# The down projection of an encoder block: tokens as rows of its result, and the last norm per row

## The chip, the core and the metric

One core of a Trainium2 chip runs the whole block; the metric is the time of one execution in microseconds. Five engines work side by side: TensorE (PE, matmuls; PEld its weight loads), VectorE (DVE), ScalarE (ACT), GpSimd (POOL) and SyncE (SP). Each works through its own list in order. Transfers between the chip's memory (SBUF) and the device memory are issued from such a list too, mostly SP's, and carried by 16 transfer engines. PSUM is where TensorE writes its sums.

## What is computed

```python
# x: (1, 2048, 1024) float32, one layer
h = rmsnorm(x, norm_mix_pre)
...                                   # input projection, two branches, gates, w_o
x = x + rmsnorm(merged @ w_o, norm_mix_post)         # "x1" in the kernel
h = rmsnorm(x, norm_mlp_pre)
f = square(relu(h @ w_up)) @ w_down                  # (2048,1024) @ (1024,4096) @ (4096,1024)
x = x + rmsnorm(f, norm_mlp_post)                    # rmsnorm over the 1024 channels of a token
```

## The kernel before

Activations lie in SBUF with channels on the 128 partitions and tokens along the row. Every float32 operand of a matmul is split in two parts of TensorE's type, a high part (a cast on ScalarE, `wh`, `fo` or `big`) and a low part (what is left, a subtraction on VectorE, `wl` or `tr`), and a product is three passes: high by high, high by low, low by high. Where a low part was made once and kept, it is loaded again instead.

The down projection (`down` in the trace) runs at the end, over four slabs `s` of 1024 hidden channels, each for two blocks `b` of 1024 tokens. A slab's product is cut in two by two halves of 512 (result channels by hidden channels by tokens) and made from seven half-size products `i` in place of eight, from sums and differences of the halves. `weights_down` makes the weights of product `i` as two tiles `o` of 128x1024; `token_cells` makes its activations as two cells (hi, lo); `down_product` runs it: for `o` in (0, 1), `product` contracts with the weight tile as the stationary operand and the cells as the moving one, 24 matmuls of 128x512 into a PSUM tile of 128x1024, whose rows are result channels and whose columns are tokens. So a weight tile is done with after its own 24 matmuls. The sums over slabs are kept in `acc` (`big` in the trace): in slab 0 ScalarE copies, later VectorE adds. The order of products is `DOWN` in slabs 0 to 2, where both blocks use one set of weights, and `DOWN_LAST` in the last slab, where it is all of b=0, then all of b=1, and where the weights are loaded again for the second block: sums from `wsum`, low parts from `lows`, both written to device memory earlier. Tiles come from pools with few buffers: three for `wh`, three for `wl`, nine for `tr`, 28 for `big`.

The last norm and the addition of x1 are the class `Finish`, one for each block b and token half t (512 tokens). Its squares are made on ScalarE (`Squares`), summed over partitions by TensorE with a column of 1/D (`root_pe`, `root_acc`, L458), the inverse root is taken on VectorE (`root_dve`), and TensorE spreads it over the partitions again (`spread_pe`, L542 and L548, tile `rb`). Then come a multiplication, an addition of x1 (on VectorE, GpSimd, or by an adding transfer) and the store of the cell. `fin[0,0]`, `fin[0,1]` and `fin[1,0]` run beside later products. The last, `fin[1,1]`, is `at_end` and `first_squares`: it follows the last product, with seven idle matmuls (L469) in between.

What sets the order: the program is written out in one list, and `Lane` objects give out steps of background work after every product half (`bg`); `high_priority` moves loads and casts ahead of their use, and `ordered` and `mark` tie the products in a row. Each engine's list follows from that, and a tile waits for its buffer to come free.

Of the kernel before, what the change touches and what calls it, by code (L numbers as in the profile page):

```python
# [45 lines left out]
C_MPOST = 40  # L46
C_CNT = 48
# [13 lines left out]
IDLE = (28, 7)  # L61
# [7 lines left out]
def block_kernel(  # L69
# [11 lines left out]
    params: bass.AP,  # L81
    out: bass.AP,
# [110 lines left out]
    fd, lod = {}, {}  # L193
# [289 lines left out]
    def root_dve(st, e=None, mean=None):  # L483
# [7 lines left out]
        if mean is not None:  # L491
            nc.vector.tensor_scalar(a, st, mean, EPS, op0=ALU.mult, op1=ALU.add)
        elif e is None:
            nc.vector.tensor_scalar(a, st, EPS, None, op0=ALU.add)
        else:
            add(a, st, e)
# [192 lines left out]
    def first_octet():  # L689
# [53 lines left out]
        with tc.high_priority(offset=URGENT), in_turn():  # L743
# [7 lines left out]
            idle(IDLE[0], root_psum())  # L751
# [815 lines left out]
    ENDS = {(1, 0): 4, (0, 0): 2, (1, 1): 5, (0, 1): 3}  # L1567
# [125 lines left out]
    chains = {}  # L1693

    def down_product(s, i, b, w, cells):
        for o in (0, 1):
            if s < LAST:
                ps = psum("down")
                product(ps, w[o], cells)
                if s == 0:  # L1700
                    acc[i, o, b] = mk(*BIG)
                    mark(nc.scalar.copy(acc[i, o, b], ps))
                else:
                    a = acc[i, o, b]
                    mark(add(a, a, ps))
            else:
                last_product(i, o, b, w[o], cells)
# [9 lines left out]
    def last_product(i, o, b, w, cells):  # L1717

        if i in (1, 2, 5):
            chains[i, o] = psum("down")  # L1720
        ps = chains[{1: 1, 6: 1, 7: 1, 4: 1, 2: 2, 5: 5, 3: 5}[i], o]
        product(ps, w, cells, start=i in (1, 2, 5), stop=i in (4, 2, 3))
        m, t = {1: (0, 0), 6: (0, 1), 7: (1, 1), 4: (1, 0), 2: (0, 0), 5: (1, 1), 3: (0, 1)}[i]
        c = acc[{(0, 0): 2, (0, 1): 3, (1, 0): 4, (1, 1): 5}[m, t], o, b]
        if (i, o, b) == (DOWN_LAST[-1], 1, 1):
            for h in (slice(0, T), slice(T, TB)):
                mark(add(c[:, h], c[:, h], ps[:, h]))
        else:
            mark(add(c, c, ps))
        if i == ENDS[m, t]:  # L1730
            fin[b, t].ready[2 * m + o] = c

    def beside(o, a, b):
        return nc.gpsimd.tensor_tensor(o, a, b, op=ALU.add)

    HOW = {(0, 0): "GGGG", (0, 1): "DGDG", (1, 0): "GGAD", (1, 1): "DDDD"}

    class Finish:


        def __init__(self, b, t):
            self.b, self.t, self.x, self.ready = b, t, {}, {}
            self.near = 4 if b else 3 if t else 1
            self.order = (2, 3, 0, 1)

        def how(self, c):
            return HOW[self.b, self.t][self.order.index(c)]

        def fetch(self, cells):
            for c in cells:  # L1750
                if self.how(c) != "A":
                    self.x[c] = mk(*BIG)
                    load(self.x[c], x1d[self.b, c, self.t])
# [267 lines left out]
```

## Time and profile before

| | us |
|---|---|
| median of 3 runs | 2172.24 (2170.28 to 2172.63) |
| profiled execution, its own time | 2174.1 |
| its span | 2172.3 |
| TensorE busy | 2144.8 |
| VectorE busy | 1706.2 |
| ScalarE busy | 1045.1 |

The span is the time from the first instruction of the profiled execution to the last; its own time has 1.8 us around that. The down projection starts near 1545 us and its last matmul ends near 2151 us. Matmuls overlap, so the durations of neighbours add up to more than the time that they take.

### The profile page before, as it was taken

What the parts mean: (1) busy time and instruction counts of PE and PEld (TensorE: products, weight loads), DVE (VectorE), ACT (ScalarE), POOL (GpSimd) and SP (SyncE); (2) the same over time, 40 slices, a digit from 0 to 9 for tenths busy, and PEclk for the clock granted to TensorE, in tenths of its full rate; (3) what the DMA queues carried; (4) which work ended last, traced back from release to release, by engine and by line L of the source; (5) the groups of instructions that cost most, each with busy time, mean ns of one, the idle gap of its engine ahead of it and who ended that gap; (6) DMA issues with size and microseconds to landing.
All of it is one profiled execution on the core that took longest, in us unless ns stands there. A gap on an engine that the chain in (4) does not pass through costs nothing.

```text
span 2172.3 us, 24919 instructions
## 1 busy us (share of the span) xinstructions
PE 2144.8 (99%) x9499; PEld 1772.5 (82%) x9499; DVE 1706.2 (79%) x1631; ACT 1045.1 (48%) x1102; POOL 40.0 (2%) x45
## 2 busy tenths in 40 slices
PE   9999999999999999999999999999999999999997
PEld 8788878888888888888888888888878888888886
DVE  8999787999779999997778856876654666597477
ACT  6444453334534655545635666665444322223453
POOL 0000000000000000000000000000000000000023
PEclk9999999999999999999999999999999999999998
DMA  4789998688897687435695777985956545446797
GB/s 177 259 304 331 337 353 314 223 293 290 304 348 285 249 304 271 153 117 223 230 351 213 269 273 288 342 312 219 364 197 232 184 169 180 155 137 206 257 361 259
DMA packets 161175, 561.21 MB, mean 258 GB/s; under 512 B 18704, under 2 KB 22928, under 8 KB 161040
## 3 DMA queue, kind: packets, MB, share of 16 engines
q1 hardware_dynamic: 144784, 500.38, 64.5%
q10 hardware_dynamic: 12672, 46.14, 5.5%
q0 software_dynamic: 3600, 13.11, 1.7%
q8 instruction: 74, 1.21, 0.2%
q14 instruction: 45, 0.37, 0.1%
HBM read 372.29 MB, written 187.79 MB: 258 GB/s over the span
## 4 chain that ended last, share of the span: by engine, by line
PE 88%; DVE 6%; DMA 2%; issue 2%; ACT 1%; SPq 0%; DVEq 0%; ACTq 0%
PE down L252 28%; PE up L252 28%; PE wo L252 7%; PE glu L252 6%; PE B L252 4%; PE gb L252 4%; PE A L252 4%; PE ga L252 3%; PE pool L252 3%; DVE y L910 3%; PE rb L458 1%; DVE tr L120 1%; DVE wl L123 1%; DMA kept<-ws 1%; DMA big<-xt 1%
## 5 line engine op out<-in xcount | busy, mean ns | idle before, releaser
L252 PE MATMUL up<-big,wh 128*128 128x512 f32 x1792 | 480.3, 390 | 1.4 <-DVE big L123 1.2
L252 PEld LDWEIGHTS up<-big,wh 128*128 128x128 f32 x1792 | 335.8, 188 | 71.9 <-DVE big L123 1.7
L209 ACT CAST wh<-wr 128x1024 fp32r<-128x1024 f32 x167 | 175.6, 1052 | 316.7 <-PE up L252 69.8
L252 PE MATMUL down<-tr,wh 128*128 128x512 f32 x800 | 311.5, 389 | 0.0
L910 DVE SCALAR_TENSOR_TENSOR y<-v,cst,y 128x1024 f32<-128x1024 f32 x240 | 306.9, 1279 | 2.4
L252 PE MATMUL down<-fo,wh 128*128 128x512 f32 x784 | 301.5, 390 | 1.1 <-ACT fo L1688 1.1
L252 PE MATMUL up<-big,wl 128*128 128x512 f32 x896 | 276.0, 389 | 0.0
L209 ACT CAST wh<-ws 128x1024 fp32r<-128x1024 f32 x124 | 130.6, 1053 | 223.9 <-PE up L252 75.0
L252 PE MATMUL down<-fo,wl 128*128 128x512 f32 x768 | 236.5, 389 | 0.0
L252 PEld LDWEIGHTS up<-big,wl 128*128 128x128 f32 x896 | 168.2, 188 | 35.0
L120 DVE TENSOR_TENSOR big<-big,down 128x1024 f32<-128x1024 f32 (+1 forms) x85 | 102.4, 1205 | 115.7 <-PE down L252 115.6
L1688 ACT CAST fo<-tr 128x1024 fp32r<-128x1024 f32 x86 | 86.8, 1051 | 207.6 <-PE down L252 139.4
L123 DVE TENSOR_TENSOR wl<-ws,wh 128x1024 fp32r<-128x1024 f32 x116 | 141.5, 1220 | 44.2 <-ACT wh L209 42.2
L252 PEld LDWEIGHTS down<-tr,wh 128*128 128x128 f32 x800 | 150.2, 188 | 31.1
L252 PEld LDWEIGHTS down<-fo,wh 128*128 128x128 f32 x784 | 147.2, 188 | 31.9 <-ACT fo L1688 1.6
L252 PEld LDWEIGHTS down<-fo,wl 128*128 128x128 f32 x768 | 144.2, 188 | 29.9
L123 DVE TENSOR_TENSOR wl<-wr,wh 128x1024 fp32r<-128x1024 f32 x111 | 135.1, 1218 | 28.1 <-ACT wh L209 23.2
L123 DVE TENSOR_TENSOR tr<-tr,fo 128x1024 fp32r<-128x1024 f32 x86 | 102.9, 1232 | 46.3 <-ACT fo L1688 46.3
L252 PE MATMUL glu<-big,wh 128*128 128x512 f32 x432 | 118.4, 396 | 3.9 <-ACT tr L408 3.9
L252 PE MATMUL gb<-big,wh 128*128 128x512 f32 x448 | 121.6, 393 | 0.2 <-ACT tr L408 0.2
L252 PE MATMUL wo<-big,wh 128*128 128x512 f32 x448 | 120.2, 390 | 0.0
L252 PE MATMUL ga<-big,wh 128*128 128x512 f32 x448 | 119.8, 389 | 0.0
(192 smaller groups left out, 3366.3 us busy)
## 6 DMA issues: line engine op xcount, KB each, us to landing
tr<-fd SPq DMA_DIRECT2D x110, 512.0 KB, 4.6
wr<-w_down SPq DMA_DIRECT2D x68, 512.0 KB, 4.8
wl<-kept SPq DMA_DIRECT2D x67, 512.0 KB, 4.8
kept<-wl SPq DMA_DIRECT2D x66, 512.0 KB, 5.5
wr<-w_up SPq DMA_DIRECT2D x64, 512.0 KB, 4.5
wr<-w_in SPq DMA_DIRECT2D x56, 512.0 KB, 5.3
fd<-tr ACTq DMA_DIRECT2D x54, 512.0 KB, 3.8
fd<-tr SPq DMA_DIRECT2D x48, 512.0 KB, 3.1
```

The lines of the kernel that those rows point to most:

```text
L120: return nc.vector.tensor_tensor(o, a, b, op=ALU.add)
L123: return nc.vector.tensor_tensor(o, a, b, op=ALU.subtract)
L209: nc.scalar.copy(hi[:, :n], src[:, :n])
L252: i = nc.tensor.matmul(ps, w[wp][:, (at + k) * P : (at + k + 1) * P], rhs[k][xp], start=start and n == 0, stop=stop and n == len(order) - ...
L458: nc.tensor.matmul(st[:, at + g : at + g + 1], ss[:, g * P : (g + 1) * P], inv_n, start=start is None or (start and g == 0), stop=stop, sk ...
L910: nc.vector.scalar_tensor_tensor(acc, v[:, k : k + TB], wk, acc, op0=ALU.mult, op1=ALU.add)
L1688: nc.scalar.copy(hi, t)
```

## The change

Products now have tokens as the rows of their result: the cells are stationary, the weights move (`token_product`). A PSUM tile holds 256 tokens (half `h`), two banks of 128 tokens by 512 channels, and both weight tiles are needed for each half: the first half reads the tiles in the order 0, 1, the second in the order 1, 0. The channels of the result are in another order (`order`), which the host undoes in the layout of `w_down`, of the gains and of the output.

A token's channels now lie along a row. So `Finish` squares and sums in one operation of ScalarE (`accum_out`) per 128 tokens and 512 channels; the root is taken on VectorE for one column per 128 tokens; a gain row, loaded once into a buffer of the pool for sums of weights (`p_ws`), is multiplied in by VectorE, and the root and x1 in one operation for 512 columns. The sums, spreads and idle matmuls on TensorE, the additions on GpSimd and the adding transfers are gone. x1 is stored with channels as rows, so `turned` loads it in pieces, transposes blocks of 32x32 on VectorE and stores it as `x1t`, in sixteen steps in slab 0; its transfers are in GpSimd's queue. `last_steps` and `at_end` are the last token half: `at_end` runs inside the last product, after each bank of 128 tokens.

```diff
+    def token_product(ps, w, cells, h, start=True, stop=True, after=None):
+        cellwise = [(j, gg) for j in ((1, 0) if h else (0, 1)) for gg in (0, 1)]
+        if after is not None:
+            cellwise = [(j, gg) for gg in (0, 1) for j in (0, 1)]
+        for n, (j, gg) in enumerate(cellwise):
+            n = [g for _, g in cellwise[:n]].count(gg)
+            at = (2 * h + gg) * P
+            for c, wp, xp in ((0, 0, 0), (0, 0, 1), (1, 0, 0), (1, 0, 1), (0, 1, 0), (1, 1, 0)):
...
+                i = nc.tensor.matmul(
+                    ps[gg],
+                    cells[j][xp][:, c * T + at : c * T + at + P],
+                    w[j][wp][:, c * T : (c + 1) * T],
...
     def down_product(s, i, b, w, cells):
-        for o in (0, 1):
+        for h in (0, 1):
             if s < LAST:
                 ps = psum("down")
-                product(ps, w[o], cells)
+                token_product(banks(ps), w, cells, h)
...
+    def turned():
+        for b in range(NB):
+            for t in (0, 1):
+                to = x1t[b, t].rearrange("(n tb i) (q k j) -> n q i tb k j", n=2, i=32, q=4, j=32)
+                for c in (0, 2):
+                    for n in (0, 1):
+                        x, y = mk(*TR), mk(*TR)
+                        s = slice(n * (T // 2), (n + 1) * (T // 2))
+                        for k in (0, 1):
+                            aside(
+                                x[:, k * T : (k + 1) * T].rearrange("p (k n) -> p k n", k=2),
+                                two(x1d[b, c + k, t])[:, :, s],
+                            )
+                        yield 2
+                        nc.vector.transpose(
...
+                        for q in range(4):
+                            aside(
+                                to[n, q][:, :, 2 * c : 2 * c + 4],
+                                y[32 * q : 32 * q + 32].rearrange("p (tb k j) -> p tb k j", k=4, j=32),
+                            )
+                        yield
...
     class Finish:
...
+        def fetch(self, g):
+            self.x[g] = mk(*BIG)
+            load(self.x[g], x1t[self.b, self.t][g * P : (g + 1) * P])
+
+        def squares(self, m, h, y, gg):
+            at = m * G + 2 * h + gg
+            nc.scalar.activation(
+                junk[0][:, :T], y, AF.Square, scale=SQ, accum_out=self.ss[:, at : at + 1]
+            )
+
+        def gain(self, m, h):
+            y = self.ready[m, h]
+            for gg in (0, 1):
+                self.squares(m, h, y[:, gg * T : (gg + 1) * T], gg)
+            row = gains[0][:, m * T : (m + 1) * T].unsqueeze(1).to_broadcast([P, 2, T])
+            mul(two(y), two(y), row)
+
+        def root(self, lo, hi):
+            ss = small("st", hi - lo)
+            add(ss, self.ss[:, lo:hi], self.ss[:, G + lo : G + hi])
+            return root_dve(ss, floor[self.b, self.t][:, lo:hi], 1.0 / D)
+
+        def cell(self, g, r, y):
+            x = self.x[g]
+            for m in (0, 1):
+                s = slice(m * T, (m + 1) * T)
+                nc.vector.scalar_tensor_tensor(x[:, s], y[m], r, x[:, s], op0=ALU.mult, op1=ALU.add)
...
+        def put(self, g):
+            (load if self.b else aside)(out[self.b, self.t, g], self.x[g])
...
+        def at_end(self, h, c, ps):
...
+            def arrive(gg):
+                s = halves[gg]
+                mark(add(c[:, s], c[:, s], ps[gg]))
+                self.squares(0, h, c[:, s], gg)
+                mul(y[:, s], c[:, s], gains[0][:, :T])
+
+            def leave(g, r):
+                to = out[self.b, self.t, g]
+                part = [y[:, halves[g % 2]], self.ready[1, h][:, halves[g % 2]]]
+                x = self.x[g]
+                for m, s in list(enumerate(halves))[::-1]:
+                    nc.vector.scalar_tensor_tensor(x[:, s], part[m], r, x[:, s], op0=ALU.mult, op1=ALU.add)
+                    load(to[:, s], x[:, s])
...
             if b == 0:
-                lanes += [Lane(3, fin[0, 0].steps(2), fin[0, 1].steps(2))]
+                gains.append(mk(p_ws, "ws"))
+                load(gains[0], post)
+                junk.append(mk(p_ws, "ws"))
+                lanes += [Lane(3, fin[0, 0].steps(3), fin[0, 1].steps(3))]
             else:
-                lanes += [Lane(2, fin[1, 0].steps(1)), Lane(2, fin[1, 1].first_squares())]
+                lanes += [Lane(2, fin[1, 0].steps(1)), Lane(2, fin[1, 1].last_steps())]
...
+        if n == 1:
+            lanes.append(Lane(2, turned()))
```

Three places show how the lists of the engines change. A name is a tile with its buffer's serial numbers; `x2` stands for two equal rows.

SP's list in the last slab, before: transfers from the load of one low part (`wl`) on; `tr` are activations, `wr` weights.

```order
L129 DMA wl_3138_15427<-lows_2230_10388 128x1024
L129 DMA tr_3127_15349<-fd_1766_8197 128x1024
L129 DMA tr_3129_15354<-fd_1821_8482 128x1024
L129 DMA wr_3175_15609<-w_down 128x1024
L129 DMA wl_3141_15433<-lows_2391_11028 128x1024
L129 DMA wr_3189_15704<-wsum_2237_10425 128x1024
L129 DMA big_3135_15421<-x1d_122_149 128x1024
L129 DMA wl_3163_15531<-lows_2301_10665 128x1024
```

The same place after the change:

```order
L129 DMA wl_3160_15423<-lows_2516_11492 128x1024
L129 DMA wl_3167_15489<-lows_2382_10952 128x1024
L129 DMA tr_3183_15584<-fd_2540_11605 128x1024
L129 DMA wr_3201_15670<-wsum_2302_10632 128x1024
L129 DMA wr_3204_15676<-wsum_2463_11272 128x1024
L129 DMA tr_3185_15589<-fd_2589_11862 128x1024
L129 DMA wl_3170_15495<-lows_2533_11568 128x1024
```

The low parts of a product's two tiles stood one or two other transfers apart and evenly; now the second tile of a product and the first of the next stand together, and four others come before the next pair.

TensorE's list in the last slab, before: the end of one weight tile (`wh_3137`, `wl_3138`) and the start of the product's other (`wh_3140`); the stationary operand stands second here.

```order
L252 MATMUL down_3146_15446<-fo_3116_15270,wl_3138_15427 128x512 x2
L252 MATMUL down_3146_15446<-big_3118_15275,wl_3138_15427 128x512
L252 MATMUL down_3146_15446<-big_3118_15275,wh_3137_15426 128x512
L252 MATMUL down_3146_15446<-tr_3117_15273,wh_3137_15426 128x512
L252 MATMUL down_3146_15446<-big_3118_15275,wl_3138_15427 128x512
L252 MATMUL down_3147_15472<-fo_3116_15270,wh_3140_15432 128x512
L252 MATMUL down_3147_15472<-tr_3115_15268,wh_3140_15432 128x512
```

After: the middle of a product's second half, where its second tile (`wl_3160`) is read for the last time and its first (`wh_3156`) is read again.

```order
L1708 MATMUL down_3134_15244<-wh_3159_15422,tr_3143_15287 128x512
L1708 MATMUL down_3134_15244<-wl_3160_15423,big_3144_15289 128x512 x2
L1708 MATMUL down_3134_15244<-wh_3156_15416,fo_3142_15284 128x512
L1708 MATMUL down_3134_15244<-wh_3156_15416,tr_3141_15282 128x512
L1708 MATMUL down_3134_15244<-wh_3156_15416,fo_3142_15284 128x512
L1708 MATMUL down_3134_15244<-wh_3156_15416,tr_3141_15282 128x512
L1708 MATMUL down_3134_15244<-wl_3157_15417,fo_3142_15284 128x512 x2
```

The first tile is now held until the product's end. The buffer of the second, `wl_3160`, is the one that the next product's second tile, `wl_3170`, gets; its first reader comes 29 matmuls after the last reader of `wl_3160`. In the order of before, the buffer of a low part of the last slab is read again 55 to 67 matmuls after its last reader.

VectorE's list at the program's end, before: the last small operations of the root, the multiplications with the spread root `rb`, the additions of x1.

```order
L522 CAST sp_16323<-sy_16321 128x4
L123 TENSOR_TENSOR sq_16324<-sy_16321,sp_16323 128x4
L126 TENSOR_TENSOR big_12191<-big_12191,rb_16327 128x1024
L126 TENSOR_TENSOR big_12218<-big_12218,rb_16327 128x1024
L126 TENSOR_TENSOR big_12565<-big_12565,rb_16327 128x1024
L1857 SCALAR_TENSOR_TENSOR big_12592<-big_12592,cst,rb_16327 128x512 x2
L120 TENSOR_TENSOR big_16208<-big_16208,big_12565 128x1024
L120 TENSOR_TENSOR big_16210<-big_16210,big_12592 128x512 x2
```

After, the same end: the add of the last bank (L120 of `rb_16262`; `rb` and `down` are PSUM tiles), its gain (L126), small operations on the roots of the last product's two halves (128x2; `st_16410` and `sa_16412` belong to the second), and four operations that make cells (L1881). Behind them stand the rest of the second root and four more of these.

```order
L120 TENSOR_TENSOR big_12652<-big_12652,rb_16262 128x512
L504 SCALAR_TENSOR_TENSOR sy_16357<-s_3321_16355,sy_16349 128x2
L126 TENSOR_TENSOR tr_16379<-big_12652,ws_15183 128x512
L126 TENSOR_TENSOR s_3323_16359<-sy_16357 128x2
L120 TENSOR_TENSOR st_16410<-ss_1853_8582 128x2
L504 SCALAR_TENSOR_TENSOR s_3324_16361<-s_3323_16359,sa_16347 128x2
L492 SCALAR_TENSOR_TENSOR sa_16412<-st_16410,e_11363 128x2
L504 SCALAR_TENSOR_TENSOR sy_16363<-s_3324_16361,sy_16357 128x2
L1881 SCALAR_TENSOR_TENSOR big_15812<-big_12202,sy_16363,big_15812 128x512
L1881 SCALAR_TENSOR_TENSOR big_15812<-tr_16314,sy_16363,big_15812 128x512
L1881 SCALAR_TENSOR_TENSOR big_15814<-big_12202,sy_16363,big_15814 128x512
L1881 SCALAR_TENSOR_TENSOR big_15814<-tr_16314,sy_16363,big_15814 128x512
```

The norm no longer starts behind the last matmul: large operations and small ones of the roots alternate, and the list from the add of the first half of product 5 on has 62 entries.

## Rows read from the trace of the kernel before

**Rows 1.** Busy time, share of the span and instructions of each engine.

```profile
PE 2144.8 (99%) x9499; PEld 1772.5 (82%) x9499; DVE 1706.2 (79%) x1631; ACT 1045.1 (48%) x1102; POOL 40.0 (2%) x45
```

**Rows 2.** Stretches: length; busy of PE, PEld, DVE, ACT, POOL; clock; DMA share; GB/s.

```profile
1565.00:1745.00 180.00, 178.09 (x784) 146.95 (x784) 94.17 (x80) 73.71 (x75) 0.00 (x0) 1.00 0.62 215
1745.00:1995.00 250.00, 250.00 (x1104) 207.10 (x1103) 179.21 (x156) 72.34 (x72) 0.00 (x0) 1.00 0.48 160
1995.00:2075.00 80.00, 80.00 (x358) 66.36 (x357) 40.40 (x45) 40.38 (x44) 0.00 (x0) 1.00 0.79 277
2075.00:2151.00 76.00, 76.00 (x352) 63.01 (x350) 63.40 (x71) 41.20 (x48) 26.20 (x15) 1.00 0.94 347
```

**Rows 3.** Chain of work that ended last, 1540 to 1620: start, length, what.

```profile
1577.27 1.01 ACT big L1702
1578.28 0.95 ACT fo L1688
...
1579.26 1.24 DVE big L123
```

**Rows 4.** Timeline of TensorE before its last matmul: start, busy, what.

```profile
2147.53 0.39 PE L252 MATMUL down<-fo,wh 128*128 128x512 f32 x1
2147.76 0.39 PE L252 MATMUL down<-tr,wh 128*128 128x512 f32 x1
...
2150.97 0.40 PE L252 MATMUL down<-big,wl 128*128 128x512 f32 x1
```

**Rows 5.** The same chain, 1990 to 2173: the norm's steps in TensorE.

```profile
2058.42 0.79 PE rb L458 x8
...
2070.26 0.46 PE rb L548 x2
...
2135.41 0.83 PE rb L458 x8
...
2138.40 1.07 PE rb L542 x8
```

**Rows 6.** Timeline of VectorE after the last matmul.

```profile
2155.67 0.16 DVE L120 TENSOR_TENSOR sa<-rb,e 128x4 f32<-128x4 f32 x1 [2.99 <-PE rb L458]
2155.87 0.17 DVE L499 TENSOR_SCALAR sy<-sa 128x4 int32<-128x4 int32 x1
...
2160.47 3.48 DVE L126 TENSOR_TENSOR big<-big,rb 128x1024 f32<-128x1024 f32 x3 [2.65 <-PE rb L542]
2163.87 1.40 DVE L1857 SCALAR_TENSOR_TENSOR big<-big,cst,rb 128x512 f32<-128x512 f32 x2
2165.18 2.72 DVE L120 TENSOR_TENSOR big<-big,big 128x1024 f32<-128x1024 f32 x3
```

**Rows 7.** The page's costliest groups: count, busy, mean ns, idle before.

```profile
L209 ACT CAST wh<-wr 128x1024 fp32r<-128x1024 f32 x167 | 175.6, 1052 | 316.7 <-PE up L252 69.8
...
L910 DVE SCALAR_TENSOR_TENSOR y<-v,cst,y 128x1024 f32<-128x1024 f32 x240 | 306.9, 1279 | 2.4
...
L123 DVE TENSOR_TENSOR wl<-wr,wh 128x1024 fp32r<-128x1024 f32 x111 | 135.1, 1218 | 28.1 <-ACT wh L209 23.2
```

**Rows 8.** Landings of low parts (lows) in both token blocks of the last slab.

```profile
DMA to landing us min/median/max: 3.4/3.9/6.3
...
DMA to landing us min/median/max: 3.9/6.5/8.7
```

**Rows 9.** Groups of VectorE by line and shape, columns as in group 7.

```profile
L919 DVE COPY sm<-y 128x1024 f32<-128x1024 f32 x2 | 1.4, 688 | 0.0
```

**Rows 10.** Groups of GpSimd by line.

```profile
L133 POOL DMA_DIRECT2D x1d<-big x8 | 4.3, 534 | 66.0 <-DVE big L120 55.3 <-DVE s L504 8.8 <-DVE s L126 1.9
```

**Rows 11.** DMA issues: count, KB each, median us to landing.

```profile
ud<-tr SPq DMA_DIRECT2D x16, 256.0 KB, 3.0
...
x1d<-big POOLq DMA_DIRECT2D x8, 512.0 KB, 6.6
x1d<-big SPq DMA_DIRECT2D x8, 512.0 KB, 5.2
```

More of the change, by code (lines that the diff above doesn't have):

```diff
@@ L192, in block_kernel @@
     )
-    fd, lod = {}, {}
+    fd, x1t = {}, {(b, t): dram("x1t", (T, D)) for b in range(NB) for t in (0, 1)}
     def col(i):
@@ L1742, in __init__ @@
             self.b, self.t, self.x, self.ready = b, t, {}, {}
[L1743 to L1753, printed above, removed]
-        def finish(self, c):
-            y, how = self.ready[c], self.how(c)
-            mul(two(y), two(y), per_token(self.rb))
-            to = out[self.b, c, self.t]
-            if how == "A":
-                nc.gpsimd.dma_start(y, x1d[self.b, c, self.t], accum_op=ALU.add)
-                nc.gpsimd.dma_start(to, y)
-                return
-            x = self.x[c]
-            (beside if how == "G" else add)(x, x, y)
-            (nc.gpsimd if how == "G" and self.b == 0 else nc.sync).dma_start(to, x)
@@ L1774, in steps @@
-            for c in self.order:
-                while c not in self.ready:
+            for k in ((0, 0), (0, 1), (1, 0), (1, 1)) if self.t == 0 else ((1, 0), (1, 1), (0, 0), (0, 1)):
+                while k not in self.ready:
                     yield 1
-                self.squares(sq, c)
+                self.gain(*k)
                 yield
-            self.fetch(self.order[: self.near])
-            ss = sq.total()
-            yield 1 if self.b else 2
-            st = root_pe(ss, inv_n=inv_d)
@@ L1801, in first_squares @@
-        def first_squares(self):
-            sq = Squares(TR)
-            for c in self.order[:2]:
-                while c not in self.ready:
-                    yield 1
-                with tc.high_priority(offset=URGENT):
-                    self.squares(sq, c)
-                yield
-            for c in self.order[:1]:
-                load(out[self.b, c, self.t], x1d[self.b, c, self.t])
-            self.fetch(self.order[1:])
-            c = self.order[2]
-            while c not in self.ready:
-                yield 1
-            with tc.high_priority(offset=URGENT):
-                sq.add(self.ready[c], SQ)
-                self.ss = sq.total()
-            gained(self.ready[c], self.ready[c], C_MPOST, c)
-            yield
@@ new lines, in steps, with last_steps @@
+            for g in range(2):
+                self.fetch(g)
+            r = self.root(0, G)
+            yield lag
+            for g in range(G):
+                if g + 2 < G:
+                    self.fetch(g + 2)
+                self.cell(g, r[:, g : g + 1], self.parts(g))
+                self.put(g)
+                yield
+        def last_steps(self):
+            for g in range(G):
+                self.fetch(g)
+            for k in ((1, 0), (1, 1)):
+                while k not in self.ready:
+                    yield 1
+                self.gain(*k)
+                yield
```

188 lines of the change are left out of this document (77 added, 111 removed).

## The prediction

> **What bounds the kernel now.** I read the busy shares first, then stretches of the down stage, then the chain that ended last, then the rows of its end. TensorE is busy in 2144.8 of 2172.3 us; VectorE has 1706.2, ScalarE 1045.1 [rows 1]. [...] So up to the last matmul the time is the number of matmuls, and anything that hides there costs nothing. Two places are different. At 1577 us the chain leaves TensorE for an eviction and a cast on ScalarE and a subtraction on VectorE [rows 3]: from 1577.27 to 1579.26 + 1.24 = 1580.50 nothing new enters TensorE, 3.2 us. And the last matmul ends at 2150.97 + 0.40 = 2151.4 [rows 4], the span at 2172.3: 20.9 us of norm and output are bare.
>
> **What the change removes in front of the last matmul.** The down products keep their number and size: 48 matmuls of 128x512 per weight pair and token block, one entering each 0.227 us (2147.53 to 2147.76) [rows 4]. What goes are the norm's sums and spreads across partitions, which stand in TensorE's stream. On the chain [rows 5]: the sums of the first two finishes 0.79 each, their spreads 0.46 each (one row of each is shown, they repeat at 2097.94 and 2109.77), then 0.83 and 1.07 for the third and 0.83 for the early part of the last: 2 x 0.79 + 2 x 0.46 + 0.83 + 1.07 + 0.83 = **5.2 us**, all of it on the path. No matmul is added.
>
> **The stop at 1577.** In the new order both casts stand ahead of that eviction on ScalarE, where now one stands behind it. What could be late next is the cells' own transfer. Between 0 and 3.2 us come back; I take the middle, **1.6**.
>
> **The end.** Now, after 2151.4, come an add, a square, sums, idle matmuls and a spread on TensorE, eleven small operations in VectorE, and eight large ones from 2160.47 on [rows 6]. In the new kernel the squares' sums come from ScalarE, per row, so TensorE isn't in it. But much more waits on VectorE: from the add of the first half of product 5 (78 matmuls, 17.7 us, before the last matmul's end) its order holds 28 operations of 512 columns, 4 of 1024 and 30 small ones. From the latter: two of 512 columns start and pass on in 2165.18 - 2163.87 = 1.31, 0.655 each; three of 1024 in 3.40, 1.13 each; a small one follows the other in 0.20. 28 x 0.655 + 4 x 1.13 + 30 x 0.20 = 28.9 us. So VectorE, not TensorE, sets the end: it is done 11.1 us after the last matmul, if it doesn't wait. From its last operation to the end of the span it takes 4.4 us now (2165.18 + 2.72 = 2167.9, 2172.3); the last output is again one of 256 KB. 15.5 in place of 20.9: **5.4 us** less. Bounds: small operations that slip between large ones may cost 0.1 (28.9 less 3.0), and waits for the squares and for x1 may add 2: a gain of 3.4 to 8.4. Because VectorE sets the end from 17.7 us before the last matmul, a wait of TensorE in that time costs nothing.
>
> **What the change takes away of cover.** A weight pair is now two tiles that both halves of the result need. The second half reads them in reverse order, so the second tile is read for the last time in the middle of that product, and its successor in the same buffer 29 matmuls later; now it is 55. 29 x 0.227 less the 0.39 of the last reader is **6.2 us** for everything that refills the buffer; before it was 12.1. In slabs 0 to 2 this is a cast of 1.05 and a subtraction of 1.22 [rows 7], 2.3 us with 3.9 over for queues: I count nothing; either engine at its worst place costs one more large operation, which fits too. In the last slab the low part is a transfer of 512 KB that waits for the buffer in SP's queue; cells, high parts and x1 are queued behind it. It landed in 3.4 to 6.3 us in the first token block, and in 3.9 to 8.7, median 6.5, in the second [rows 8]. Against 6.2 that is 0 in the first and 0.3 (median) to 2.5 (worst) for each of seven in the second; the last is free, as said. The new queue has an advantage: after each low part of a first tile come about 8 us in which other transfers drain; it has also a place where nine stand in a row. I take 1.0 each, nearer to the median: 6 x 1.0 = **6.0 us** of waits, bounds 0 and 15. [...]
>
> **x1 turned on the chip.** This is new work of sixteen steps in the first slab: two loads of 256 KB and four stores of 128 KB each on GpSimd's queue, and a VectorE transpose between. 16.8 MB over the 180 us are 93 GB/s on top of 215, together 308, below the 347 that the last stretch carries with TensorE full [rows 2]. A transpose isn't in the trace; between a copy of that size at 0.69 [rows 9] and the dearest pass at 1.28 [rows 7] it is 11 to 20 us of VectorE, which is idle for 86 of these 180. On the path I count 0; the bound above is the third rival. Squares, gains and last multiplications of the first three finishes move from one place of VectorE and ScalarE to another and hide under full TensorE; GpSimd's additions go.
>
> **Sum.** The profiled execution's own time is 2174.1 (span 2172.3 and 1.8 around it), 1.9 above the median of the runs, 2172.24. 2174.1 - 5.2 - 1.6 - 5.4 + 6.0 = 2167.9; less 1.9: **2166**.
>
> **Rivals.** (1) The low parts are in time. For it: the same transfer takes 3.4 to 4 us whenever nothing is queued ahead, and the reordered queue leaves gaps. Against it: 0.94 of the transfer engines in the second block. It gives 2160. (2) They are late in both blocks, which makes it slower. TensorE waits at the second tile's low part in each product of the last slab: 12 that aren't free, up to 8.7 - 6.2 = 2.5 each, 30 us: 2190. It decides from a mean landing of 6.2 + 12.2 / 12 = 7.2 us. For it: the 8.7 [rows 8] with nearly the same traffic. Against it: the first block's 6.3 at worst. (3) The turn paces the first slab. GpSimd's queue is in order: landing of the second load, the transpose (1.2), then five issues of 0.53 [rows 10] until the next step's second load, per step of 48 matmuls, 10.9 us. It decides from a landing of 10.9 - 1.2 - 2.7 = 7.0. The rows of transfers give 3.0 for 256 KB on SP, 5.2 and 6.6 for the same 512 KB on SP and on GpSimd [rows 11]. With the 8.7 of a crowded queue a step is 1.7 too long, 16 of them 27 us, less a lead of 26 matmuls (5.9): 21 us, 2187. What passes it on is VectorE, which stands at the transpose in order, with the weights' low parts behind it. [...] (4) The end gains nothing: VectorE is late already when its list begins, or waits for x1 there. It gives 2166 + 5.4 = 2171. A change that does less than it says isn't likely otherwise: the removed matmuls are gone from the order.
>
> **How the numbers follow.** About 0.2%, 4.3 us, can be told from no change. Forecast 0.36 (own range 2162 to 2172; 0.26 of it faster, 0.10 same); first rival 0.25, faster; second 0.20 (0.16 slower, 0.04 same, where waits are half as long); third 0.11 (0.08 and 0.03); fourth 0.08 (0.06 same, 0.02 slower). Faster 0.51, same 0.23, slower 0.26. The range reaches from 2159 (no waits, a little more at the end) to 2184, which leaves out the longer halves of the second and third rival.
>
> **What would show it.** Right: no rows of sums or spreads between down products from 2030 us on; TensorE's waits in the last slab are for transfers into wl, some 6 us in all and nearly all in the second token block; the last matmul near 2146 + 4; VectorE without gaps from there, its last operation some 11 us after the last matmul. Wrong: waits for wl in the first block too (second rival), waits of VectorE at the transposes and of TensorE in the first slab (third), VectorE idle in the last 15 us before the last matmul, or a gap of over 18 us between last matmul and end (fourth). What I can least defend is the 1.0 us per low part.

## The result

The changed kernel takes 2175.1 us in the median of 20 runs (2169.66 to 2182.45), the kernel before 2170.86 in 20 runs beside it (2167.59 to 2173.54): a ratio of 1.0022, 95% interval 1.0015 to 1.0029. It is slower by 0.2%, where 2166, faster than before, was forecast. The time lies in the stated range, on the slow side.

The profiled execution took 2174.9 with a span of 2173.1, only 0.8 more than the span of before. But the down projection began 5.2 us earlier in it. I take that as chance: in the traces of the changed kernel and of its eleven variants below, which are the same up to there, it begins at 1536.8 to 1544.1. The first matmul of the down products, in the timeline of TensorE (start us, busy us, what) of the kernel before:

```profile
1544.43 0.39 PE L252 MATMUL down<-fo,wh 128*128 128x512 f32 x1
```

and of the changed kernel:

```profile
1539.21 0.39 PE L1708 MATMUL down<-wh,fo 128*128 128x512 f32 x1
```

From there to the end of the span it is 2172.3 - 1544.4 = 627.9 before and 2173.1 - 1539.2 = 633.9 after. These 6.0 us are what the two traces have to explain.

### The profile page after: what moved, and what is told of

Read it like the earlier page. It is cut to its first block, busy times and chain, and to the rows that moved or that the text cites. A ratio compares the mean times of both kernels' runs of the same rounds, so it can differ in the third digit from the quotient of the medians.

```text
span 2173.1 us, 25018 instructions
## 1 busy us (share of the span) xinstructions
PE 2135.3 (98%) x9424; PEld 1759.1 (81%) x9424; DVE 1716.1 (79%) x1664; ACT 1034.3 (48%) x1119; POOL 74.8 (3%) x131
## 4 chain that ended last, share of the span: by engine, by line
PE 73%; DVE 9%; DMA 9%; issue 5%; ACT 2%; POOL 1%; SPq 0%; DVEq 0%; ACTq 0%; POOLq 0%
PE up L252 28%; PE down L1708 18%; PE wo L252 7%; PE glu L252 5%; PE B L252 4%; PE ga L252 3%; PE gb L252 3%; DVE y L910 3%; PE pool L252 2%; DMA tr<-x1d 2%; PE A L252 2%; DMA wl<-lows 1%; DMA tr<-fd 1%; POOL x1t L133 1%; DVE wl L123 1%
## 5 line engine op out<-in xcount | busy, mean ns | idle before, releaser
L1708 PE MATMUL down<-wh,tr 128*128 128x512 f32 x784 | 307.0, 392 | 3.2 <-DVE tr L123 3.2
L1708 PE MATMUL down<-wh,fo 128*128 128x512 f32 x776 | 298.6, 390 | 0.5 <-ACT wh L209 0.5
L1708 PE MATMUL down<-wl,fo 128*128 128x512 f32 x760 | 235.1, 391 | 3.0 <-DVE wl L123 3.0
L1708 PEld LDWEIGHTS down<-wh,tr 128*128 128x128 f32 x784 | 148.0, 189 | 35.2 <-DVE tr L123 4.3
L1708 PEld LDWEIGHTS down<-wh,fo 128*128 128x128 f32 x776 | 145.9, 188 | 31.4 <-ACT wh L209 0.9
L1708 PEld LDWEIGHTS down<-wl,fo 128*128 128x128 f32 x760 | 142.7, 188 | 34.6 <-DVE wl L123 5.3
L120 DVE TENSOR_TENSOR big<-big,down 128x1024 f32<-128x1024 f32 (+1 forms) x84 | 99.8, 1189 | 70.4 <-PE down L1708 70.3
```

The lines of the kernel that those rows point to most:

```text
L120: return nc.vector.tensor_tensor(o, a, b, op=ALU.add)
L1708: i = nc.tensor.matmul(ps[gg], cells[j][xp][:, c * T + at : c * T + at + P], w[j][wp][:, c * T : (c + 1) * T], start=start and first, stop ...
```

## The profile after

The page's line of busy times, which answers to [rows 1]:

```profile
PE 2135.3 (98%) x9424; PEld 1759.1 (81%) x9424; DVE 1716.1 (79%) x1664; ACT 1034.3 (48%) x1119; POOL 74.8 (3%) x131
```

TensorE has less to do and the span is no shorter. The same stretches as in [rows 2], in the same columns:

```profile
1565.00:1745.00 180.00, 174.54 (x755) 142.07 (x755) 101.96 (x87) 69.59 (x70) 52.20 (x83) 0.99 0.80 271
...
1995.00:2075.00 80.00, 79.28 (x350) 65.32 (x349) 41.56 (x44) 38.88 (x57) 0.00 (x0) 1.00 0.83 300
2075.00:2151.00 76.00, 68.70 (x290) 55.65 (x289) 48.10 (x69) 29.20 (x47) 4.34 (x8) 0.96 0.86 325
```

Before, TensorE was full in all of them but for 1.9 us in the first; now it is short of full by 5.5 us in the first and by 7.3 in the last. The transfer engines rose from 0.62 to 0.80 in the first slab, and the clock fell in the last token block. What TensorE waited for from the start of the down products to the end, from the view of waits (us in total, times, longest):

```profile
PE down L1708 <- DMA wl<-lows: 8.0, 3, 6.2
PE down L1708 <- DVE tr L123: 3.2, 2, 1.8
PE down L1708 <- DVE wl L123: 3.0, 4, 1.3
PE down L1708 <- ACT wh L209: 0.5, 1, 0.5
```

So 6.7 us are waits for VectorE and ScalarE, all between 1640 and 1761, and 8.0 are three waits for low parts of weights. The rows of TensorE's weight loads have 10.1 and 9.3 for the same stops (at 2128.25 they have 6.59 where the matmuls have 6.17); I take the cost to lie between.

**First slab.** The longest of the waits there, first in the timeline of VectorE of the changed kernel (in brackets, the idle time before and what ended it):

```profile
1651.27 1.25 DVE L1784 STREAM_TRANSPOSE tr<-tr 128x1024 f32<-128x1024 f32 x1 [3.32 <-DMA tr<-x1d]
1652.44 1.18 DVE L123 TENSOR_TENSOR tr<-tr,fo 128x1024 fp32r<-128x1024 f32 x1
```

and in that of TensorE:

```profile
1653.68 0.50 PE L1708 MATMUL down<-wh,tr 128*128 128x512 f32 x1 [1.80 <-DVE tr L123]
```

VectorE had nothing to do for 3.32 us, because the next entry in its list was the transpose and its input was not there. Behind it stood the low part of a cell (1652.44), and TensorE waited 1.80 for that. The loads of the turn themselves land in 4.9 us in the median. They are issued late, and the reason stands in the timeline of GpSimd in the changed kernel ahead of this transpose:

```profile
1638.32 1.76 POOL L133 DMA_DIRECT2D x1t<-tr  x3 [3.54 <-DVE tr L1784]
1643.42 0.58 POOL L133 DMA_DIRECT2D x1t<-tr  x1 [3.34 <-issue]
1645.35 0.71 POOL L133 DMA_DIRECT2D tr<-x1d  x1 [1.35 <-issue]
1647.22 0.73 POOL L133 DMA_DIRECT2D tr<-x1d  x1 [1.16 <-DVE tr L123]
```

and, for the whole turn, in its waits:

```profile
POOL x1t L133 <- issue: 57.0, 22, 5.3
```

Three of a step's four stores go out; in front of the fourth GpSimd stands for 3.34 us, for nothing that the profile names, and the two loads of the next step come behind. There are 22 such stops before stores, 57.0 us in sum; a step takes 13.2 us in the mean (from 1550.9 to 1749.3 in fifteen steps) in place of 10.9.

When these stops end can be read from the landings. The store that was issued at 1638.32 has, in the view of its tile,

```profile
DMA to landing us min/median/max: 4.8/4.8/4.8
```

so it lands at 1643.1, and the fourth store starts at 1643.42. It is so throughout this trace: of the 24 stops of over 0.8 us that the profile gives no cause for, all end within 0.35 us of the landing of an earlier GpSimd transfer, with three under way until then, and no transfer of the turn is issued while three earlier ones are under way. Why is not shown, and three is not shown to be a bound: two transfers of 512 KB, earlier in the program (694.4 and 716.8), were issued with three under way, after idle times of 0.0 and 0.1 us.

There is a second way by which the turn is passed on. SP's own waits from 1565 to 1765 have

```profile
SPq L129 <- DMA x1t<-tr: 71.0, 15, 10.5
```

These are loads that need a buffer which the turn holds until its stores have landed. Without the turn (e1) there is no such wait. The last of TensorE's seven waits, 1.26 us at 1760, comes after the last transpose (1747.7) and behind a cell's load for which ScalarE had stood 8.54 us. How the seven waits divide between the two ways, the runs don't show.

**Last token block.** SP's timeline in the changed kernel ahead of the longest wait:

```profile
2107.35 0.32 SPq L129 DMA_DIRECT2D wl<-lows  x1
2107.71 0.43 SPq L129 DMA_DIRECT2D big<-x1t  x1
2108.24 0.87 SPq L129 DMA_DIRECT2D wr<-wsum  x2
2109.16 1.40 SPq L129 DMA_DIRECT2D big<-x1t  x2
2110.66 1.19 SPq L129 DMA_DIRECT2D wr<-wsum  x2
2113.07 1.54 SPq L129 DMA_DIRECT2D big<-x1t  x2
2115.76 3.04 SPq L129 DMA_DIRECT2D wl<-lows  x2
```

The chain of work that ended last, in order of time (start us, us, what), has the landing of the low part issued at 2115.76:

```profile
2115.76 12.44 DMA wl<-lows
2128.25 14.31 PE down L1708 x50
```

The timeline of TensorE then:

```profile
2121.69 0.39 PE L1708 MATMUL down<-wh,tr 128*128 128x512 f32 x1
2128.25 1.22 PE L1708 MATMUL down<-wl,big 128*128 128x512 f32 x2 [6.17 <-DMA wl<-lows]
...
2134.18 0.40 PE L1708 MATMUL down<-wh,big 128*128 128x512 f32 x1
```

Two short stretches, before and after the clock rose again (columns as in [rows 2]):

```profile
2128.00:2130.00 2.00, 1.75 (x4) 1.46 (x5) 1.04 (x1) 0.00 (x0) 0.53 (x1) 0.50 0.93 377
...
2134.00:2138.00 4.00, 4.00 (x19) 3.30 (x18) 1.23 (x1) 1.82 (x4) 0.00 (x0) 1.00 0.30 89
```

Between two low parts SP issued nine other transfers of 512 KB in 8 us: five of x1 and four of raw weights. The low part behind them landed after 12.4 us, and TensorE stood for 6.17. Then its granted clock was 0.50 until 2134: 14 matmuls in 5.93 us, which at 0.227 are 3.18, so 2.75 more. In the first slab the same happened once, after waits of 0.48 and 1.40 with one matmul between them, from 1690.1 to 1694.0: nine matmuls in 3.85 in place of 2.04, 1.8 more, with the clock at 0.57 in the mean from 1690 to 1694. After the wait of 1.80 above it was 1.00 (1652 to 1656).

VectorE stood in the same place, a little earlier, at a cell of x1 from the same row of transfers:

```profile
2119.12 2.74 DVE L1831 SCALAR_TENSOR_TENSOR big<-big,sy,big 128x512 f32<-128x512 f32 x4 [7.83 <-DMA big<-x1t]
```

TensorE's wait for the low part hid this stop; e6 and e8 bring it out.

**The end.** The last matmuls in the changed kernel's timeline of TensorE:

```profile
2159.61 0.61 PE L1708 MATMUL rb<-wl,big 128*128 128x512 f32 x2
```

and, where [rows 6] stood before, the first and the last of VectorE's list that was counted in the prediction:

```profile
2142.58 0.69 DVE L120 TENSOR_TENSOR big<-big,down 128x512 f32<-128x512 f32 x1
...
2168.75 0.75 DVE L1881 SCALAR_TENSOR_TENSOR big<-tr,sy,big 128x512 f32<-128x512 f32 x1
```

The last matmul ends at 2160.2, VectorE at 2169.5, the span at 2173.1: 12.9 us after the last matmul, where it was 20.9.

**The stop at 1577.** The changed kernel has no wait there. What the stop of [rows 3] cost before is read from TensorE's timeline of the kernel before:

```profile
1577.75 0.39 PE L252 MATMUL down<-big,wh 128*128 128x512 f32 x1
1579.28 0.49 PE L252 MATMUL down<-fo,wh 128*128 128x512 f32 x1 [1.14 <-ACT fo L1688]
1580.54 0.50 PE L252 MATMUL down<-big,wh 128*128 128x512 f32 x1 [0.77 <-DVE big L123]
```

Two matmuls took 2.79 us to follow where two at 0.227 take 0.45, so it was 2.3 us and not the 3.2 of the chain, during which some matmuls still went in.

The sum of it, from the first down product to the end: -5.2 for the norm's rows, -2.3 for that stop, -8.0 at the end; +14.7 to +19.4 of waits, +4.6 of slow clock. That is +3.8 to +8.5; the traces differ by 6.0.

## The experiments

Each ran beside the kernel before, whose medians there were 2170.4 to 2171.0. The last column is the time from the first down product to the end of the last, in the one execution that was traced; it leaves out the chance of the part ahead. Executions of one kernel differ by 4 to 13 us, so medians a few us apart with overlapping intervals are not told apart.

| run | median, us | ratio to before (95%) | first to last down product |
|---|---|---|---|
| kernel before | 2170.86 | | 606.9 |
| changed kernel | 2175.1 | 1.0022 (1.0015 to 1.0029) | 621.0 |
| e1 no turn | 2164.55 | 0.9975 (0.9964 to 0.9986) | 608.7 |
| e2 turn every third half | 2172.27 | 1.0008 (0.9999 to 1.0018) | 616.0 |
| e3 low parts on GpSimd | 2200.91 | 1.0132 (1.0111 to 1.0153) | 649.7 |
| e4 x1 late | 2172.05 | 1.0009 (0.9997 to 1.0020) | 618.4 |
| e5 more lead for the turn | 2164.33 | 0.9960 (0.9946 to 0.9975) | 609.4 |
| e6 four buffers for low parts | 2173.07 | 1.0007 (0.9996 to 1.0019) | 619.6 |
| e7 = e5 and e4 | 2158.43 | 0.9933 (0.9919 to 0.9948) | 602.1 |
| e8 = e5 and e6 | 2163.47 | 0.9957 (0.9944 to 0.9970) | 606.3 |
| e9 = e5, e4 and e6 | 2158.62 | 0.9943 (0.9930 to 0.9957) | 600.9 |
| e10 = e7, x1 one cell earlier | 2161.67 | 0.9953 (0.9938 to 0.9969) | 606.5 |
| e11 stores of the turn on SP | 2170.25 | 1.0003 (0.9992 to 1.0014) | 618.2 |

### e1: without the turn

```diff
         if n == 1:
-            lanes.append(Lane(2, turned()))
+            pass
...
-            load(self.x[g], x1t[self.b, self.t][g * P : (g + 1) * P])
+            load(self.x[g], x1d[self.b, g, self.t])
```

> The changed kernel without its sixteen turning steps: the last norm reads x1 as it is stored (channels as rows), so the x1 that it adds is in the wrong order, and nothing else is left out. Theory A (in the changed kernel's profile TensorE waits 6.7 us for VectorE and ScalarE between 1640 and 1715, all behind the turn, and 8.0 us for low parts in the last slab, and its granted clock halves after the longest wait): those 6.7 go, with the slow clock after them some 7.5, so 2175.1 - 7.5 = about 2167.5; the waits for low parts stay. Rival B (the turn only covers waits that are there without it, the stop of 3.2 us of the kernel before among them): about 2171 or more.

It took 10.55 us less, more than theory A's 7.5. TensorE's waits left in e1, from the start of the down products on:

```profile
PE down L1708 <- DMA wl<-lows: 7.1, 2, 5.8
PE down L1708 <- DVE big L123: 0.4, 1, 0.4
```

All of the first slab's waits but 0.4 are gone, and that 0.4 stands at 1577, where the kernel before has its stop. Rival B is out: the turn alone costs 10.6 in the median, and the waits for low parts are there without it.

### e2: the same turn at a slower pace

```diff
-            lanes.append(Lane(2, turned()))
+            lanes.append(Lane(1, turned()))
```

> The same sixteen turning steps, handed out every third product half in place of every second, 16.3 us apart in place of 10.9: same transfers, same VectorE work, nothing left out. Theory A1 (the pace: GpSimd's queue needs some 13 us for a step, so VectorE stands at a transpose whose input is late): the waits in slab 0 go and it is as without the turn, about 2167.5. Rival A2 (the work itself: 16.8 MB more traffic and 20 us more VectorE in front of the weights' low parts): most of the waits stay, above 2172.

2172.27: theory A1, the pace, fails, and what rival A2 forecast came, if barely: above 2172, and of the 6.7 us of waits behind the turn 5.9 are left (four of seven). VectorE stood at three transposes, for 11.4 us, and SP for the turn's stores only 9.0 us, where it was 71.0. A step now had 16.3 us, but the time between its loads and its transpose was still two product halves. That pointed to the lead; whether it is rival A2's work itself, e5 decides.

### e5: more lead

```diff
-                        yield 2
+                        yield 4
                         nc.vector.transpose(
```

> The changed kernel with four product halves in place of two between the loads of a turning step and its transpose, so a step every 21.8 us; nothing left out. In the run with steps of 16.3 us TensorE still waited 5.9 us behind the turn. Theory A1 (the lead: the loads stand in GpSimd's queue behind stores that it can't issue for 4 us, and VectorE, in order, stands at the transpose): no wait behind the turn is left and the time is that of the kernel without it, 2164.5, up to 2166. Rival A2 (the added VectorE work and 16.8 MB of traffic cost something wherever they are): 2168 or more.

2164.33, the time of e1, with all the turn's work in it. The transposes of e5, by their line (duration in ns min/median/max), and the one idle time ahead of them:

```profile
L1784 DVE STREAM_TRANSPOSE tr<-tr x16: 1235/1238/1245, 1553.2 to 1909.7; 128x1024 f32<-128x1024 f32 x16
...
  DMA tr<-x1d: 2.9, 1
```

It waited once, 2.9 us, in place of eight times and 29.6, and TensorE never. Theory A1 holds: 16.8 MB of transfers and 20 us of VectorE cost nothing that can be told once nobody stands in line for them. Rival A2 is out. The stops of GpSimd are still there,

```profile
POOL x1t L133 <- issue: 56.0, 14, 5.3
```

so it is not their going that helps. But the edit does two things: it doubles the lead, and a step comes every 21.8 us in place of 10.9. A pace of 16.3 alone (e2) was not enough; the pace of 21.8 with the old lead was not run, so lead and pace are not told apart.

### e11: the stores of the turn on SP

```diff
                         for q in range(4):
-                            aside(
+                            load(
                                 to[n, q][:, :, 2 * c : 2 * c + 4],
```

> The changed kernel (two halves between load and transpose) with the 64 stores of the turned x1 in SP's queue in place of GpSimd's, the 32 loads still in GpSimd's; nothing left out. Theory A1 (GpSimd stands 57 us in front of these stores, 22 times, in the changed kernel, and the next step's loads stand behind them): the stops of GpSimd go, the loads are issued in time, the waits in slab 0 fall under 3 us and the time to 2167 or less. Rival (16.8 MB more at the same time make loads late whatever queue holds them, or SP, in order, now stands at the stores and the weights behind them are late): 2173 or more.

2170.25: 4.9 less, where theory A1 wanted 8 or more and the rival 2 at most. GpSimd's loads, from 1565 on, stand before no issue without a cause (three stops, 14.0 us, come before 1557); they wait for their buffers, as its waits in e11 have it:

```profile
POOL tr L133 <- DVE tr L1784: 90.3, 7, 17.4
```

So the stops of the turn came with its stores in GpSimd's queue. But TensorE still waited 6.4 us there, for casts and low parts of cells. SP's list is in order too, and its 64 more entries cost it 16.8 us of waits for transposes and 14.4 for stores to land; that this made the cells late is likely, but not shown apart.

### e3: low parts of the last slab on GpSimd

```diff
-                load(f32(lo), lows[i, o])
+                aside(f32(lo), lows[i, o])
                 return hi, lo
```

> The changed kernel with the low parts of the last slab's weights issued by GpSimd in place of SP, nothing else. Theory C1 (they are late because others are queued ahead of them in SP's queue, nine for the one that landed after 12.4 us): they land in 4 to 6 us, waits for wl fall from 8.0 to under 2 us and the slow clock after the long one goes: 2175.1 - 6 - 2.7 = about 2166. Rival C2 (the transfer engines are full, 0.86 to 0.95 there, whatever the queue): landings above 8 us stay and the time with them, 2173 or more.

The worst of all: 25.8 us slower than the changed kernel. The landings of all low parts of the last slab in the changed kernel:

```profile
DMA to landing us min/median/max: 3.4/4.6/12.4
```

the same in e3:

```profile
DMA to landing us min/median/max: 3.6/7.5/8.8
```

and TensorE's waits for them in e3:

```profile
PE down L1708 <- DMA wl<-lows: 16.6, 9, 4.9
```

The worst landing is better (8.8 for 12.4), but the median went from 4.6 to 7.5, over the 6.2 that a second tile has; nine waits in place of three. So theory C1 failed as it was put: here a queue of its own did not let a transfer overtake.

The queue was not quite its own, though. GpSimd's list also has the eight output stores of the first token block, and the low parts stand behind them. Its timeline in e3 ahead of the longest of the nine waits:

```profile
2152.16 0.54 POOL L133 DMA_DIRECT2D out<-big  x1 [6.19 <-DVE big L1831]
2152.78 1.15 POOL L133 DMA_DIRECT2D wl<-lows  x2
```

GpSimd had stood 6.19 us for the cell that it was to store, and the low part behind it, issued at once, landed at 2160.5, when TensorE had waited 4.94. So e3 mixes two things, longer landings and an in-order list with stores in it.

What made the median 7.5 is not shown; a transfer of 512 KB took longer from GpSimd than from SP before the change too (6.6 against 5.2 [rows 11]).

### e4: x1 of the last token half later

```diff
         def last_steps(self):
-            for g in range(G):
-                self.fetch(g)
...
+        def late_fetch(self):
+            yield 9
+            for g in range(G):
+                self.fetch(g)
+                yield 1
...
-                lanes += [Lane(2, fin[1, 0].steps(1)), Lane(2, fin[1, 1].last_steps())]
+                lanes += [Lane(2, fin[1, 0].steps(1)), Lane(2, fin[1, 1].last_steps()), Lane(2, fin[1, 1].late_fetch())]
```

> The changed kernel with the four loads of x1 for the last token half later and one at a time, so that five and not nine transfers stand between the low parts around 2115 us; nothing left out. Theory C1 (what is queued ahead): the landing of 12.4 us falls to about 7, the wait of 6.2 to under 1.5, and the clock stays up: 2175.1 - 5 - 2.7 = about 2167.5, less up to 2 if x1 comes late for the last cells. Rival C2 (bandwidth of the whole stretch): the wait moves to another low part and stays 5 us or more in sum, 2173 or more.

2172.05, between the two and nearer to C2's 2173. No low part was late any more (6.2 us at worst in the last block), but TensorE waited 2.63 for the low part of a cell, with slow clock behind it (0.66 in the mean from 2115 to 2125). The timeline of VectorE of e4 in that place:

```profile
2112.81 1.41 DVE L1831 SCALAR_TENSOR_TENSOR big<-big,sy,big 128x512 f32<-128x512 f32 x2 [3.50 <-DMA big<-x1t]
...
2115.27 2.35 DVE L123 TENSOR_TENSOR tr<-tr,big 128x1024 fp32r<-128x1024 f32 x2
```

It stood 3.50 us at a cell of x1, whose transfer took 10.8, and the cell's low part came behind. This is rival C2's wait, in a smaller form and at another tile. With five transfers between the low parts in place of nine the worst landing fell, 6.2 for 12.4, as C1 has it, but the time goes to the next in the row. The execution in the profile took 2174.9, more than the median; it had 8.4 us of waits behind the turn, where that of the changed kernel had 6.7.

### e6 and e8: four buffers for low parts

```diff
-                hi, lo = mk(p_wh, "wh", F32R), mk(p_wl, "wl", F32R)
+                turn[0] += o
+                hi = mk(p_wh, "wh", F32R)
+                lo = mk(p_wr, "wr", F32R) if o and turn[0] % 2 else mk(p_wl, "wl", F32R)
```

> The changed kernel with every second low part of a second weight tile of the last slab in a buffer of the pool of raw weights (five buffers), so that the low parts have four buffers and none must be refilled within 29 matmuls; nothing left out. Theory D1 (the short time in which a buffer is refilled is the cause of the waits in the last slab): no wait for a low part, and 2175.1 - 8.0 - 2.7 = about 2165. Rival D2 (the last slab's second token block has the transfers of some 10 us ahead of whatever is needed next, so another tile is late in its place, x1 for VectorE or a cell's part): a wait of 3 us or more for VectorE and slow clock behind it, 2171 or more.

> Four halves between load and transpose, and low parts in four buffers; nothing left out. Theory D1: 2175.1 - 10.6 - 10.7 = about 2154, faster than either kernel. Rival D2: about 2162.

2173.07, and 2163.47 with the lead of e5, which is not told apart from e5. No wait for a low part is left, and nearly as much of another. TensorE's waits in e8, the whole of them:

```profile
PE down L1711 <- DVE big L120: 5.6, 1, 5.6
```

and the timeline of VectorE there:

```profile
2111.64 1.42 DVE L1834 SCALAR_TENSOR_TENSOR big<-big,sy,big 128x512 f32<-128x512 f32 x2 [9.30 <-DMA big<-x1t]
...
2119.21 3.48 DVE L120 TENSOR_TENSOR big<-big,down 128x1024 f32<-128x1024 f32 x3
```

VectorE stood 9.30 us at x1; the additions that empty PSUM (2119.21) came after, and TensorE waited 5.6 for a free tile, with slow clock behind it (0.95 in the mean from 2075 to 2145, where e7 below has 1.00; the 12 matmuls from 2120.48 on took 4.53 us, which at 0.227 are 2.72). This stop of VectorE was there before (7.83 in the changed kernel), under the wait for the low part. Theory D1, the step that the prediction built on, is out as a price: with more than 29 matmuls to refill a buffer, the low part is in time and the time is the same. With e4 this says that what costs is the row of transfers ahead of whatever is needed next.

### e7, e9 and e10: both, and what is left

e7 has the edits of e5 and e4, e9 those of e5, e4 and e6; e10 is e7 with

```diff
-            for g in range(2):
+            for g in range(3):
                 self.fetch(g)
...
-                if g + 2 < G:
-                    self.fetch(g + 2)
+                if g + 3 < G:
+                    self.fetch(g + 3)
```

> Both together: four halves between load and transpose, and x1 for the last token half fetched late, one load at a time; nothing left out. If the costs are separate they add: 2175.1 - 10.6 - 3.0 = about 2161.5. If the wait for x1 in the last slab was only seen because slab 0 had lost time, it would give more, 2157.

> Four halves between load and transpose, x1 of the last token half fetched late, and low parts of the last slab in four buffers; nothing left out. Without the buffers TensorE still waited 1.7 us for a cell's low part (VectorE stood at a late x1) and 0.9 for low parts of weights. Theory D1 (buffers matter once the burst is gone): 2158.4 - 0.9 = about 2157.5. Rival D2 (only what stands in SP's queue ahead of the next needed tile matters): 2158.4 within 1, or slower, since one buffer fewer is left for raw weights.

> Four halves between load and transpose, x1 of the last token half late, and in the other three token halves x1 fetched three cells ahead in place of two; nothing left out. In the run with two ahead VectorE stood 9.1 us at x1 in the last slab, and one such stop reached TensorE as 1.7 us. If it is the lead of x1 that is short: 2158.4 - 1.7 = about 2156.5. If an earlier x1 only takes the place of another transfer in SP's queue: 2158 to 2161.

e7 takes 2158.43, 16.7 us under the changed kernel and 0.67% under the kernel before. TensorE's waits in e7, in the whole down projection:

```profile
PE down L1708 <- DVE tr L123: 1.7, 1, 1.7
PE down L1708 <- DMA wl<-lows: 0.9, 2, 0.5
```

This is more than the gains of e5 and e4 together, 10.8 + 3.1, and nearer to the 2157 of the second reading; the traces say the same (18.9 less from first to last down product, against 11.7 + 2.6). A reason stands in them: the wait of 2.63 in e4 had slow clock behind it (0.95 in the mean from 2075 to 2145), and the 1.7 here had not (1.00). e9 is the same within what can be told (D2 again). e10's median is 3 us higher, with overlapping intervals; its trace has less waiting of VectorE for x1 (6.3 us in place of 9.1) and more of TensorE for low parts (3.4 in place of 0.9), as its second reading has it.

## Why the prediction was wrong

**The norm's rows, 5.2, and the stop at 1577, 1.6.** Both right in direction. No sum or spread stands between the down products any more. Of the stop all or nearly all came back (0.4 is left in e1), but it was 2.3 and not 3.2: the prediction read the chain as if nothing entered TensorE meanwhile. In e7 the time from the first to the last down product is 602.1 against 606.9, less by 4.8; -5.2 - 2.3 + 2.6 of waits are -4.9.

**The end, 5.4.** Right mechanism, too small: 8.0. VectorE's list did begin 17.6 us before the last matmul's end and had no gap worth the name, but took 26.9 in place of 28.9; by the prediction's own prices for the large ones that leaves 0.13 for each small one, in place of 0.20; and the end of the span came 3.6 after its last operation in place of 4.4. The bounds held.

**The low parts, 6.0.** Mis-sized and wrongly shaped. I spread 1.0 over each of six; measured were three waits of 8.0 in sum, one of them 6.2, and 2.75 of slow clock: 10.8. (The list of before that is shown has three and two other transfers between its low parts, not one or two.) The prediction had seen the place where nine transfers stand in a row, and then gave it the same 1.0 as the others. Priced by the stretch, with 0.94 of the transfer engines at 347 GB/s [rows 2], ten times 512 KB are 15 us, less some 8 in which they are issued: a landing of 7 to 15, and a wait of up to 9. That is an estimate, and its 8 is from the trace after. And the short time for refilling was not the price: with a fourth buffer the wait went to another tile (e6).

**x1 turned on the chip, 0.** The step that failed most: 10.6 (e1 against the changed kernel). The third rival had it, and how it is passed on: VectorE stands at the transpose, with the weights' and cells' low parts behind it. Its condition was wrong: it asked whether a load lands within 7.0 us. The loads landed in 4.9, and were late all the same, since they were issued late. The term that failed is the five issues of 0.53, 2.7 us for a step, from rows in which GpSimd had issued eight single transfers [rows 10]: GpSimd stood 57 us in front of the stores besides, 3.6 for each step, and its stops of over 0.8 ended within 0.35 us of the landing of an earlier transfer. Landing 4.9, transpose 1.2, issues 2.7 and these 3.6 are 12.4, over the 10.9 of a step. Two product halves of lead didn't cover that; four, at half the pace, did (e5). The wait of SP for the turn's buffers (71.0) was in no rival. With 11 in 100 for that rival, the doubt was in the right place and too small.

**The clock.** Not in the sum: 4.6 us after two of the waits (2.75 and 1.8, with the clock at 0.50 and 0.57). Here a price for waits of TensorE has to hold it.

**Chances.** The second and the third rival were taken as alternatives to the forecast. They are separate mechanisms in separate stages; both came in part, and their costs added to some 21 (10.6 and 10.8) against a gain of 15.5 (5.2, 2.3 and 8.0). The low parts alone would have left the kernel faster (e5, 2164.3). That was a fault of the reckoning, not of the profile.

## What to carry to other kernels

Background work on an idle engine was free here once nothing in that engine's list waited for its input (e5: 2164.33, where the changed kernel took 2175.1): give its loads enough lead, and count the stops of the queue that issues them and the buffers that it holds, not only the landing. Where a queue is nearly full, price its worst run of neighbours (here a landing of 12.4 us), not its median (4.6); here another buffer only chose who waits (e8), and another queue made it worse (e3). Independent risks add: reckon them in one sum and not as rivals of which one comes true.

## What the runs showed of the hardware

- In the changed kernel no transfer of the turn (128 and 256 KB) was issued with three earlier ones of GpSimd under way. GpSimd made 22 stops without a named cause before its stores, 57.0 us in sum and up to 5.3 each, and all those of over 0.8 ended within 0.35 us of a landing. With the stores on SP it had no such stop from 1565 to 1765 (e11).
- A transpose of 32x32 blocks in 128x1024 of float32 took 1.24 us on VectorE, as much as an addition of that size (1.22).
- After a wait of 6.17 us TensorE's granted clock was 0.50, and 14 matmuls took 5.93 us in place of 3.18. The length of a wait alone didn't say here whether the clock falls: after single waits of 1.80 (changed kernel) and 2.57 (e2) matmuls followed each other in 0.23, after one of 2.63 (e4) in 0.43; after waits of 0.48 and 1.40 with one matmul between them in 0.43, after 1.13 and 0.76 (e2) in 0.23.
- A low part issued from GpSimd landed in 7.5 us in the median (e3), one in SP's crowded queue in 4.6.
